# Output projection with head scales folded into the loaded operand, and the MLP's first operands made in pieces

## The chip, the core and the metric

The kernel runs on one core of one Trainium2 chip. The metric is the device time of one execution in microseconds (us). The core's engines run side by side, each through its own queue in order: TensorE (PE, with its weight loads PEld), VectorE (DVE), ScalarE (ACT), GpSimd (POOL), and SyncE (SP), which issues DMAs.

## The reference

One encoder block on 2048 tokens of width 1024, in float32: RMSNorm and input projection; on half of the width differential attention (4 heads), on the other half Fourier mixing; output projection with residual; RMSNorm and a gated MLP with a convolution over positions; a final RMSNorm. What concerns the change:

```python
o_da = diff_attention(q, k, v, lam, slopes)
o_da = rmsnorm(o_da, g_subln[l], SUBLN_EPS) * (1.0 - lambda_init)   # one scale per token and head
o_ft = fourier_mix(u, w_ft[l])
mixed = jnp.concatenate([o_da.reshape(B, S, DA_WIDTH), o_ft], axis=-1)
x = x + mixed @ w_out[l]
h = rmsnorm(x, g_ffn[l])
up = centred_dwconv(h @ w_up[l], w_conv[l], b_conv[l])
```

## The kernel before, in words

A product of float32 operands is made of three matmuls: `split` (L77) writes an operand as a high part (ACT) and a low part (a subtraction on DVE, or on POOL for the operand `ms`), and `mm3` (L119) runs high x high (L125), high x low (L126) and low x high (L127) into one PSUM bank.

**Attention** (L531) runs over 64 units, a head h and 128 queries i, in 4 steps t each. A step issues four score matmuls `s` (L567), four transposes `pt` (L598) of an earlier unit, and six value matmuls `o`. DVE takes the scores out of PSUM (L572), ACT makes the exponentials, POOL combines the two softmaxes (`combine`, L579: L441, L444 and two additions L589 for a unit). Two units are a pair `pr`. When a pair's `o` is complete, `finish` (L611) stores it unscaled in the DRAM tensor `mixed`, and two steps later makes the head scale: two matmuls with a column of ones (L624), a product on DVE (L629, `ft`), and on POOL L630, L631 (a power) and L632, which writes the column into the constant tile `fs` [token, head, block]. Nothing reads `fs` before the output projection. POOL also issues the loads of `q` (L504), one for every four units.

**The output projection** (`out_proj`, L693) runs over 16 blocks `tb` of 128 tokens. `load` (L709) brings a block of `mixed` (`mt`; half 1 is the Fourier part, half 0 the heads), splits it into `ms` (high on ACT, low on POOL), and brings the residual `x`. For each half of the output columns, `half` (L721) runs one group of 12 matmuls for the Fourier part (`of`), added by DVE (L733), and then four groups of three matmuls, one for each head (`o`), each added by DVE times that head's column of `fs` (L738). `close` (L741) of the block before makes the norm: square on ACT (L95), L98 and L100 on POOL (`h_rs`), product on DVE (L691, `hn`); its PE transposes (L754, `ht`) stand between the two parts of the next block's second half, and ACT copies (L758) and stores them in the DRAM tensor `htd`. `ms` has three buffers: the low part of a block's head half can be made only when the Fourier group of the block before has been run a second time.

**The MLP's first operands.** Its first group of products (tokens 0 to 1023) takes sums and differences of four quarters of `htd`, for four row groups `kb`. `b_part` (L806) makes them inside the output projection, after blocks 9, 11, 12 and 14: two loads of 512 KB into the one staging tile `hb`, four sums on POOL (L796 to L799), splits of four results into `b` (high ACT, low DVE) and copies of two on POOL into `held` (L825).

The order on each engine is not the order of the code alone: the framework places the instructions of independent parts by its own estimate of when each can start, and every engine then runs its list strictly in that order. A wait of an engine's head holds all that stands behind it.

Of the kernel before, what the change touches and what calls it, by code (L numbers as in the profile page):

```python
# [11 lines left out]
F32 = mybir.dt.float32  # L12
F32R = mybir.dt.float32r
# [7 lines left out]
P = 128  # L21
D = 1024
S = 2048
# [17 lines left out]
class Block:  # L41
# [3 lines left out]
    def __init__(self, ctx, tc, a):  # L45
# [22 lines left out]
        self.gd = dt("gd", [NF, P, S], F32)  # L68

# [461 lines left out]
    def attention(self, pss):  # L531

        nc, a = self.nc, self.a
        with ExitStack() as es:
# [98 lines left out]

            self.wo = {}
# [22 lines left out]
            for t in range(4 * (NU + LAG + 4)):  # L657
# [29 lines left out]


# [4 lines left out]
    def out_proj(self, big, operands):  # L693
# [3 lines left out]
        with ExitStack() as es:  # L697
# [11 lines left out]
            def load(tb):  # L709
                ms = []  # L710
                for half in (1, 0):
                    mt = p.tile([P, 4, P], F32, tag="mt", bufs=3, name=f"mt{tb}_{half}")
                    nc.sync.dma_start(mt, self.mixed[4 * half:4 * half + 4, :, tb * P:(tb + 1) * P].rearrange("k p t -> p k t"))
                    m2 = p.tile([P, 4, 2, P], F32R, tag="ms", bufs=3, name=f"ms{tb}_{half}")
                    self.split(mt, m2[:, :, 0, :], m2[:, :, 1, :], lo_engine=nc.gpsimd)
                    ms.insert(0, m2)
                x2 = p.tile([P, D], F32, tag="xh", name=f"x2_{tb}")
                nc.sync.dma_start(x2, a["x"][tb * P:(tb + 1) * P, :])
                ready[tb] = ms, x2

            def half(tb, half, between=None):  # L721
# [4 lines left out]

                def group(kbs, name):
                    ps = pso.tile([P, HALF], F32, tag="o", name=f"{name}{tb}_{half}")
                    return ps, self.mm3(ps, [term(kb) for kb in kbs])

                f = lambda h: self.fs[:, h, tb:tb + 1]
                ps, mm = group(range(H, KB), "of")
                nc.vector.tensor_tensor(x2[:, c], ps, x2[:, c], ALU.add)  # L733
                if between is not None:
                    between(mm)
                for h in range(H):
                    ps, _ = group([h], f"o{h}_")
                    last = nc.vector.scalar_tensor_tensor(x2[:, c], ps, f(h), x2[:, c], ALU.mult, ALU.add)  # L738
                return last

            def close(tb, behind=None):  # L741
                ms, x2 = ready.pop(tb)
                hn = p.tile([P, D], F32, tag="xh", name=f"hn{tb}")
                r = self.norm(p, hn, x2, gffn, f"h{tb}", hn)
                if behind is not None:
                    self.issue_after(r, behind)
# [59 lines left out]
    def b_part(self, grp, kb, out):  # L806

# [5 lines left out]
        for half in range(2):  # L813
# [5 lines left out]
        t1, t2, t3, t4 = self.sums(self.sp, (x11, x21, x12, x22), f"hs{grp}_{kb}",  # L819
                                   nc.vector if grp else nc.gpsimd, True)  # L820
        for o, v in zip(out, (x11, t1, t2, x21, t3, t4, x22)):
            if o is None:
                continue
            if len(o.shape) == 3:
                nc.gpsimd.tensor_copy(o[:, kb], v)  # L825
            else:
                self.split(v, o[:, 0, kb], o[:, 1, kb])
# [197 lines left out]
    def ffn(self, es_k):  # L1025
        nc, a = self.nc, self.a
        with ExitStack() as es:
# [6 lines left out]
            with ExitStack() as est:  # L1034
                late = self.pool(est, "late", 1)
                held = [late.tile([P, 4, HALF], F32, tag=f"h{i}", name=f"held{i}") for i in range(2)]
                self.out_proj(self.big, lambda step: self.b_part(0, step, self.bops + held + [None]) )
# [112 lines left out]
```

## Time and profile before

| what | us |
|---|---|
| median of 3 runs (2570.17 to 2577.55) | 2571.42 |
| the profiled execution's own time | 2574.7 |
| its span | 2572.9 |
| attention without Fourier work beside it | from about 440 to 979 |
| output projection | 979 to 1204 |

The profile page gives for each engine its busy time and share of the span, and the busy share in 40 slices of 64.3 us (a 9 is 90% or more). DVE is busy for 1752.6 us (68%), ACT for 1301.9 us (51%). Other views list instructions in order of time, who waited for whom, the chain of work that ended last, and busy times in chosen stretches. In a row `out<-in` names what an instruction writes and reads, buffer numbers left out; of a matmul's two operands the names are those of its operands, weights and moving data.

### The profile page before, as it was taken

What the parts mean: (1) busy time and instruction counts of PE and PEld (TensorE: products, weight loads), DVE (VectorE), ACT (ScalarE), POOL (GpSimd) and SP (SyncE); (2) the same over time, 40 slices, a digit from 0 to 9 for tenths busy, and PEclk for the clock granted to TensorE, in tenths of its full rate; (3) what the DMA queues carried; (4) which work ended last, traced back from release to release, by engine and by line L of the source; (5) the groups of instructions that cost most, each with busy time, mean ns of one, the idle gap of its engine ahead of it and who ended that gap; (6) DMA issues with size and microseconds to landing.
All of it is one profiled execution on the core that took longest, in us unless ns stands there. A gap on an engine that the chain in (4) does not pass through costs nothing.

```text
span 2572.9 us, 34950 instructions
## 1 busy us (share of the span) xinstructions
PE 2516.6 (98%) x13021; PEld 2114.6 (82%) x13021; DVE 1752.6 (68%) x2691; ACT 1301.9 (51%) x2036; POOL 716.9 (28%) x797
## 2 busy tenths in 40 slices
PE   9999999999999999978999999999999999999998
PEld 9998877888888888866888888877888888888886
DVE  4533358988889996786877777657777777434443
ACT  6321246888888883233544454444454445333332
POOL 1300015888988883271010010000000000000000
PEclk9999999999999999988999999999999999999999
DMA  8335558343332205554222221454212222546463
GB/s 264 98 125 139 152 143 237 66 74 73 74 75 50 48 26 173 181 174 140 107 74 79 88 79 70 160 181 155 91 74 76 88 83 85 185 137 219 146 204 113
DMA packets 146154, 309.12 MB, mean 120 GB/s; under 512 B 12080, under 2 KB 69440, under 8 KB 138816
## 3 DMA queue, kind: packets, MB, share of 16 engines
q1 hardware_dynamic: 90816, 226.60, 26.2%
q0 software_dynamic: 18256, 34.57, 6.7%
q10 hardware_dynamic: 36912, 45.72, 5.8%
q8 instruction: 102, 1.67, 0.3%
q14 instruction: 68, 0.56, 0.1%
HBM read 225.05 MB, written 81.80 MB: 119 GB/s over the span
## 4 chain that ended last, share of the span: by engine, by line
PE 87%; DVE 5%; DMA 4%; issue 1%; POOL 1%; ACT 1%; SPq 0%; POOLq 0%; ACTq 0%; DVEq 0%
PE s L567 9%; PE pd L127 5%; PE pd L125 5%; PE pd L126 5%; PE pt L598 4%; PE o L125 3%; PE o L127 3%; PE o L126 3%; PE pz L125 2%; PE pz L127 2%; PE pz L126 2%; DMA hb<-htd 2%; PE pv L127 1%; PE pv L126 1%; PE pv L125 1%
## 5 line engine op out<-in xcount | busy, mean ns | idle before, releaser
L589 POOL TENSOR_TENSOR z<-z,z 128x1024 f32<-128x1024 f32 x128 | 307.1, 2414 | 0.1
L82 DVE TENSOR_TENSOR d<-wd,d 128x512 fp32r<-128x512 f32 x240 | 157.0, 689 | 211.7 <-ACT d L81 211.4
L567 PE MATMUL s<-k,q 128*128 128x512 f32 x1024 | 281.5, 396 | 3.0 <-DVE mn L572 2.0
L576 ACT ACTIVATE z<-z,mn 128x2048 f32<-128x2048 f32 x128 | 257.5, 2012 | 33.7 <-DVE mn L572 32.7
L81 ACT ACTIVATE d<-wd 128x512 fp32r<-128x512 f32 x240 | 141.8, 626 | 236.9 <-PE pd L127 186.2
L125 PE MATMUL pd<-d,d 128*128 128x512 f32 x640 | 251.8, 393 | 1.9 <-ACT d L81 1.4
L127 PE MATMUL pd<-d,d 128*128 128x512 f32 x640 | 251.2, 393 | 0.5 <-DVE d L82 0.5
L126 PE MATMUL pd<-d,d 128*128 128x512 f32 x640 | 251.5, 393 | 0.0
L567 PEld LDWEIGHTS s<-k,q 128*128 128x128 f32 x1024 | 174.5, 188 | 29.4 <-DVE mn L572 5.0
L572 DVE CUSTOM_DVE_ANT_0 z<-s,dist,mn 128x1024 f32<-128x1024 f32 x128 | 163.8, 1280 | 38.6 <-PE s L567 37.8
L82 DVE TENSOR_TENSOR at<-pt,at 128x512 fp32r<-128x512 f32 x256 | 169.9, 686 | 8.5 <-ACT at L81 8.4
L81 ACT ACTIVATE at<-pt 128x512 fp32r<-128x512 f32 x256 | 147.5, 592 | 48.2 <-PE pt L598 44.8
L125 PE MATMUL o<-at,v 128*128 128x256 f32 x512 | 162.0, 316 | 0.0
L598 PE MATMUL pt<-ident,z 128*128 128x128 f32 x1024 | 156.7, 276 | 5.1 <-DVE at L82 5.1
L572 DVE CUSTOM_DVE_ANT_0 z<-s,dist 128x1024 f32<-128x1024 f32 x128 | 155.8, 1217 | 5.4 <-PE s L567 4.4
L598 PEld LDWEIGHTS pt<-ident,z 128*128 128x128 f32 x1024 | 125.7, 144 | 36.3 <-issue 10.5
L98 POOL TENSOR_SCALAR y_rs<-y_rs 128x1 f32<-128x1 f32 x16 | 6.9, 429 | 524.9 <-ACT sq L95 524.9
L126 PE MATMUL o<-at,v 128*128 128x256 f32 x512 | 146.3, 286 | 0.0
L125 PEld LDWEIGHTS pd<-d,d 128*128 128x128 f32 x640 | 120.1, 188 | 30.6 <-ACT d L81 1.8
L127 PEld LDWEIGHTS pd<-d,d 128*128 128x128 f32 x640 | 120.1, 188 | 29.0 <-DVE d L82 1.4
L127 PE MATMUL o<-at,v 128*128 128x256 f32 x512 | 143.7, 281 | 0.0
L126 PEld LDWEIGHTS pd<-d,d 128*128 128x128 f32 x640 | 120.1, 188 | 27.7 <-DVE d L82 0.3
(1058 smaller groups left out, 6895.0 us busy)
## 6 DMA issues: line engine op xcount, KB each, us to landing
wu<-in_w_up SPq DMA_DIRECT2D x44, 1024.0 KB, 4.8
wd<-in_w_down SPq DMA_DIRECT2D x88, 512.0 KB, 3.6
wd<-gd SPq DMA_DIRECT2D x88, 256.0 KB, 3.9
q<-qd POOLq DMA_DIRECT2D x32, 512.0 KB, 7.0
gd<-t SPq DMA_DIRECT2D x22, 512.5 KB, 2.6
gd<-t SPq DMA_DIRECT2D x22, 511.5 KB, 3.1
wst<-in_w_in SPq DMA_DIRECT2D x72, 128.0 KB, 3.6
xt<-in_xt SPq DMA_DIRECT2D x16, 512.0 KB, 4.6
```

The lines of the kernel that those rows point to most:

```text
L81: r = nc.scalar.activation(hi, src, AF.Copy)
L82: return r, (lo_engine or nc.vector).tensor_tensor(lo, src, hi.bitcast(F32), ALU.subtract)
L98: nc.gpsimd.tensor_scalar(t[:, 1:2], t[:, 0:1], 1.0 / D, EPS, ALU.mult, ALU.add)
L125: mm(ah, bh, start=first and i == 0, stop=False)
L126: mm(ah, bl, start=False, stop=False)
L127: r = mm(al, bh, start=False, stop=last and i == n - 1)
L567: nc.tensor.matmul(ps[:, j * HALF:(j + 1) * HALF], qt[:, 2 * c + l, i % 4 * P:i % 4 * P + P], kt[:, c, k0:k0 + HALF], start=l == 0, stop=l ...
L572: nc.vector.tensor_tensor_reduce(zt[:, half * 1024:(half + 1) * 1024], ps, dist[:, d0:d0 + 1024], SLOPES[h], 3.0e38 if half == 0 else mn[: ...
L576: nc.scalar.activation(zt, zt, AF.Exp, bias=mn[:, 2 * c + 1:2 * c + 2], scale=-1.0, accum_out=ss[:, c:c + 1])
L589: nc.gpsimd.tensor_tensor(z[:, x], z[:, x], z1[:, x], ALU.add)
L598: nc.tensor.transpose(pt[:, j * P:(j + 1) * P], zs[n, 0][:, kb * P:(kb + 1) * P], self.ident)
```

## The change

1. The scale rows. Behind every second pair, four columns of `fs` (four blocks of one head) are transposed on PE into a free part of that pair's PSUM bank, copied by DVE and stored by SP into a new DRAM tensor `fsd` [head, token]. The last four come in the output projection, at block 1.
2. `load` brings the four rows of `fsd` for its block to all partitions (`fr`, one buffer) and POOL multiplies `mt` of the heads by them before the split.
3. `half` runs all 24 matmuls into one bank and DVE adds it once; the 128 instructions of L738 are gone. `close` of the block before stands before the first half, and its norm no longer waits behind that half's last DVE instruction.
4. `b_part` for the first group becomes the generator `b_pieces`: loads, sums and splits in 14 pieces, one before and one behind each second half from block 9 on, and two staging tiles in turn. The sums of the first group stay on POOL.

```diff
+            def scale_rows(pr):
+                h, i = units[2 * pr]
+                if i % 4 == 2 and 2 * pr + 2 < NU:
+                    self.scale_rows(op, pos[pr][:, W + P:], h, i - 2)
...
+                if v >= 14 and (v - 14) % 8 == 0 and (v - 14) // 8 < NU // 2:
+                    scale_rows((v - 14) // 8)
...
+    def scale_rows(self, p, pt, h, i):
+        nc = self.nc
+        nc.tensor.transpose(pt[:4, :P], self.fs[:, h, i:i + 4], self.ident)
+        st = p.tile([4, P], F32, tag="fsr", bufs=1, name=f"fsr{h}_{i}")
+        nc.vector.tensor_copy(st, pt[:4, :P])
+        nc.sync.dma_start(self.fsd[h, i * P:(i + 4) * P].rearrange("(n p) -> n p", p=P), st)
...
+                    if half == 0:
+                        fr = p.tile([P, 4, P], F32, tag="fr", bufs=1, name=f"fr{tb}")
+                        nc.sync.dma_start(fr, self.fsd[:, c].partition_broadcast(P))
+                        nc.gpsimd.tensor_tensor(mt, mt, fr, ALU.mult)
...
-                ps, mm = group(range(H, KB), "of")
-                nc.vector.tensor_tensor(x2[:, c], ps, x2[:, c], ALU.add)
+                ps = pso.tile([P, HALF], F32, tag="o", name=f"o{tb}_{half}")
+                mm = self.mm3(ps, [term(kb) for kb in range(H, KB)], last=False)
                 if between is not None:
                     between(mm)
-                for h in range(H):
-                    ps, _ = group([h], f"o{h}_")
-                    last = nc.vector.scalar_tensor_tensor(x2[:, c], ps, f(h), x2[:, c], ALU.mult, ALU.add)
-                return last
+                self.mm3(ps, [term(kb) for kb in range(H)], first=False)
+                return nc.vector.tensor_tensor(x2[:, c], ps, x2[:, c], ALU.add)
...
             for tb in range(NB):
-                last = half(tb, 0)
-                transposes = close(tb - 1, last) if tb > 0 else None
+                transposes = close(tb - 1) if tb > 0 else None
+                half(tb, 0)
+                if tb == 1:
+                    self.scale_rows(p, pst.tile([P, HALF], F32, tag="tp", name="fsr"), H - 1, NB - 4)
                 if tb + 1 < NB:
                     load(tb + 1)
+                if tb > 8:
+                    next(pieces, None)
                 half(tb, 1, transposes)
-                if tb in (9, 11, 12, 14):
-                    operands((9, 11, 12, 14).index(tb))
+                if tb > 8:
+                    next(pieces, None)
...
+    def b_pieces(self, out):
...
+            for i in range(4):
+                nc.sync.dma_start(st[kb][i], self.htd[kb + 4 * (i % 2), :, i // 2 * HALF:(i // 2 + 1) * HALF])
+        load(0)
+        load(1)
+        yield
+        for kb in range(4):
+            x11, x21, x12, x22 = st[kb]
+            t1, t2, t3, t4 = self.sums(self.sp, (x11, x21, x12, x22), f"hs0_{kb}", nc.gpsimd, True)
+            yield
+            for n, (o, v) in enumerate(zip(out, (x11, t1, t2, x21, t3, t4))):
+                if n == 3:
+                    yield
+                if len(o.shape) == 3:
+                    nc.gpsimd.tensor_copy(o[:, kb], v)
+                else:
+                    self.split(v, o[:, 0, kb], o[:, 1, kb])
+            if kb + 2 < 4:
+                load(kb + 2)
+            yield
```

How the instructions stand on the engines, at three places. Lines of the changed kernel are one or more higher than those of before for the same statement (L598 is L599, L82 is L83, L796 to L799 are L813 to L816, L825 is L865).

First PE in attention, at the step where a second pair's rows are taken (here pair 3). Before:

```order
L567 MATMUL s_00_5489<-k_4054,q_3_5179 128x512 x4
L125 MATMUL o_5350<-at_3_5272,v_4314 128x256
L598 MATMUL pt_0_5495<-ident,z_0_5288 128x128 x4
L126 MATMUL o_5350<-at_3_5272,v_4314 128x256
L127 MATMUL o_5350<-at_3_5272,v_4314 128x256
```

And now:

```order
L568 MATMUL s_00_5494<-k_4055,q_3_5184 128x512 x4
L699 MATMUL o_5152<-ident,fs 4x128
L599 MATMUL pt_0_5504<-ident,z_0_5293 128x128 x4
L126 MATMUL o_5355<-at_3_5277,v_4315 128x256
L127 MATMUL o_5355<-at_3_5277,v_4315 128x256
```

The transpose of `fs` (L699) stands directly behind the four score matmuls of that step, ahead of the transposes and of everything else on PE; it reads the column that POOL's L632 (now L633) wrote for the same pair. There are 15 such places, all with the same neighbours but the last.

Second PE where the output projection begins, now:

```order
L128 MATMUL o_10844<-at_3_10779,v_8350 128x256
L625 MATMUL o_10844<-ones,osq_10910 128x1 x2
L699 MATMUL fsr<-ident,fs 4x128
L126 MATMUL o_0_10983<-wo_x_9177,ms_1_10970 128x512
L127 MATMUL o_0_10983<-wo_x_9177,ms_1_10970 128x512
L128 MATMUL o_0_10983<-wo_x_9177,ms_1_10970 128x512
```

The sixteenth transpose stands here, though the code has it at block 1: behind the last two ones matmuls (L625) and ahead of the first matmul of the output projection. Before, the ones matmuls were followed by that matmul.

Third POOL, from the norm of block 8 (`h_rs`) on. The low part of the head half of block 10 is `ms_0_11871` before and `ms_0_11818` now. Before:

```order
L100 TENSOR_TENSOR h_rs<-h_rs,mhalf 128x1
L796 TENSOR_TENSOR hs_0_t_11929<-hb_0_11926 128x512
L797 TENSOR_TENSOR hs_0_t_11930<-hb_0_11926,hs_0_t_11929 128x512
L798 TENSOR_TENSOR hb_0_11926<-hb_0_11926 128x512
L799 TENSOR_TENSOR hs_0_t_11931<-hb_0_11926,hs_0_t_11930 128x512
L825 COPY held_10884<-hb_0_11926 128x512
L825 COPY held_10885<-hs_0_t_11931 128x512
L82 TENSOR_TENSOR ms_0_11871<-mt_0_11869,ms_0_11871 128x4x128
```

And now, from the third sum of row group 0 on (the first two stand directly ahead):

```order
L815 TENSOR_TENSOR hb_0_11823<-hb_0_11823 128x512
L816 TENSOR_TENSOR hs_0_t_11878<-hb_0_11823,hs_0_t_11877 128x512
L865 COPY held_10945<-hb_0_11823 128x512
L734 TENSOR_TENSOR mt_0_11921<-mt_0_11921,fr_11923 128x512
L865 COPY held_10946<-hs_0_t_11878 128x512
L813 TENSOR_TENSOR hs_1_t_12036<-hb_11_11829,hb_10_11828 128x512
L814 TENSOR_TENSOR hs_1_t_12037<-hb_11_11829,hs_1_t_12036 128x512
L815 TENSOR_TENSOR hb_11_11829<-hb_11_11829 128x512
L816 TENSOR_TENSOR hs_1_t_12038<-hb_10_11828,hs_1_t_12037 128x512
L865 COPY held_10945<-hb_11_11829 128x512
L83 TENSOR_TENSOR ms_0_11818<-mt_0_11813,ms_0_11818 128x4x128
```

Twelve instructions (two row groups' sums, three copies and the product for block 11) now stand between the norm of block 8 and block 10's low part, where six stood before. Behind it follow a copy, the four sums of row group 2, the low part of block 11's Fourier half, two copies, and only then the norm of block 9; then, with the product for block 12 among them, the four sums and two copies of row group 3, and the low part of block 11's head half. The pieces that the code hands out over blocks 9 to 15 thus stand on POOL in blocks 9 to 11.

More of the change, by code (lines that the diff above doesn't have):

```diff
@@ L691, in norm, with out_proj @@
         return self.nc.vector.scalar_tensor_tensor(hn, x2, r, gain, ALU.mult, ALU.mult)
-    def out_proj(self, big, operands):
+    def out_proj(self, pieces):
         nc, a = self.nc, self.a
@@ L725, in half, with close @@
                                    wo[kb][:, 0, c], wo[kb][:, 1, c])
[L727 to L731, printed above, removed]
-                ps, mm = group(range(H, KB), "of")
-                nc.vector.tensor_tensor(x2[:, c], ps, x2[:, c], ALU.add)
+                ps = pso.tile([P, HALF], F32, tag="o", name=f"o{tb}_{half}")
+                mm = self.mm3(ps, [term(kb) for kb in range(H, KB)], last=False)
                 if between is not None:
                     between(mm)
-                for h in range(H):
-                    ps, _ = group([h], f"o{h}_")
-                    last = nc.vector.scalar_tensor_tensor(x2[:, c], ps, f(h), x2[:, c], ALU.mult, ALU.add)
-                return last
-            def close(tb, behind=None):
+                self.mm3(ps, [term(kb) for kb in range(H)], first=False)
+                return nc.vector.tensor_tensor(x2[:, c], ps, x2[:, c], ALU.add)
+            def close(tb):
                 ms, x2 = ready.pop(tb)
                 hn = p.tile([P, D], F32, tag="xh", name=f"hn{tb}")
-                r = self.norm(p, hn, x2, gffn, f"h{tb}", hn)
-                if behind is not None:
-                    self.issue_after(r, behind)
+                self.norm(p, hn, x2, gffn, f"h{tb}", hn)
                 nc.scalar.dma_start(self.x2d[tb], x2)
@@ L817, in b_part, with load @@
         x11, x21, x12, x22 = (st[:, i] for i in range(4))
-        t1, t2, t3, t4 = self.sums(self.sp, (x11, x21, x12, x22), f"hs{grp}_{kb}",
-                                   nc.vector if grp else nc.gpsimd, True)
+        t1, t2, t3, t4 = self.sums(self.sp, (x11, x21, x12, x22), f"hs{grp}_{kb}", nc.vector, True)
         for o, v in zip(out, (x11, t1, t2, x21, t3, t4, x22)):
[L822 to L825, printed above, removed]
-            else:
-                self.split(v, o[:, 0, kb], o[:, 1, kb])
+            self.split(v, o[:, 0, kb], o[:, 1, kb])
+    def b_pieces(self, out):
+        nc = self.nc
+        st = {}
+        def load(kb):
+            if kb % 2 == 0:
+                t = self.sp.tile([P, 4, HALF], F32, tag="st", bufs=1, name=f"hb0_{kb}")
+                st[kb] = [t[:, i] for i in range(4)]
+            else:
+                t = [self.sp.tile([P, 2, HALF], F32, tag=f"a{i}", bufs=1, name=f"hb0_{kb}{i}") for i in range(2)]
+                st[kb] = [t[i // 2][:, i % 2] for i in range(4)]
+            for i in range(4):
[13 more added lines that the diff above has]
+                else:
+                    self.split(v, o[:, 0, kb], o[:, 1, kb])
+            if kb + 2 < 4:
+                load(kb + 2)
+            yield
     def stage(self, name):
```

10 lines of the change are left out of this document (7 added, 3 removed).

## Prediction

> **What bounds the kernel now.** I read the page first. Columns: engine, busy time, share of the span, instructions; below, busy tenths in slices of 64.3 us.
>
> ```profile
> PE 2516.6 (98%) x13021; PEld 2114.6 (82%) x13021; DVE 1752.6 (68%) x2691; ACT 1301.9 (51%) x2036; POOL 716.9 (28%) x797
> PE   9999999999999999978999999999999999999998
> POOL 1300015888988883271010010000000000000000
> ```
>
> PE is the bound, and full in all but a few slices. So an edit gains only where PE stands still, and loses wherever it makes PE stand still. PE's holes (7 and 8) lie in the second part of the output projection. Attention (slices 7 to 15) has none, and POOL is busiest there. The busy times by stretch cut the output projection in two (stretch, length, PE, PEld, DVE, ACT, POOL, granted clock, DMA share, GB/s):
>
> ```profile
> 979.00:1087.00 108.00, 108.00 (x500) 87.43 (x500) 76.20 (x100) 29.41 (x52) 30.57 (x37) 1.00 0.54 164
> 1087.00:1204.00 117.00, 94.05 (x398) 75.66 (x397) 86.08 (x102) 35.20 (x60) 55.34 (x56) 0.90 0.52 164
> ```
>
> Until block 9 PE has no hole, whatever DVE does. After that it loses 23 us, and its clock falls to 0.90. The chain of work that ended last, in order of time, tells how much and why:
>
> ```profile
> 1011.05 0.90 PE ht L754 x8
> ...
> 1071.38 0.90 PE ht L754 x8
> ...
> 1085.16 3.80 DMA htd<-hs
> 1088.97 6.57 DMA hb<-htd
> ...
> 1194.46 0.89 PE ht L754 x8
> ```
>
> The transposes of successive blocks stand one period apart: five periods from 1011.05 to 1071.38, so 12.07 us for a block, or (12.07 - 0.90) / 48 = 0.233 for a matmul. The next eight take 123.08 instead of 96.5: **26.5 us is all that the operand work costs there**, stops and half clock together. The path goes through `hb`, loaded 3.8 + 6.57 us after block 7 is stored, then through POOL and ACT queues that hold `ms` and `hn` behind the sums.
>
> **Part by part.** *Head scales out of the evictions.* These groups are from the output projection:
>
> ```profile
> L738 DVE SCALAR_TENSOR_TENSOR x<-o,fs,x 128x512 f32<-128x512 f32 x128 | 95.9, 749 | 19.4 <-PE o L127 9.0
> L691 DVE SCALAR_TENSOR_TENSOR hn<-x,h_rs,gffn 128x1024 f32<-128x1024 f32 x16 | 23.3, 1456 | 2.3 <-POOL xg L892 2.2
> ```
>
> DVE loses 95.9 us of work. I cost this at nothing: in the first stretch PE ran 108.00 of 108.00 us beside it, so PE was its cover and there was no stop to recover. PE still has 24 matmuls a half; fewer PSUM groups change no count.
>
> *Scale rows in attention.* Fifteen times PE takes a transpose of `fs` right behind the score matmuls, and waits there for POOL's L632 of the same pair. The list in order of time, at pairs 1, 2, 3, 23 and 27 (start, duration); the PE rows are what PE did next after those scores:
>
> ```profile
> 485.99 0.60 PE L598 MATMUL pt<-ident,z 128*128 128x128 f32 x4
> 488.01 0.18 POOL L632 TENSOR_TENSOR fs<-ft,rr 128x2 f32<-128x2 f32 x1
> ...
> 498.55 0.20 POOL L632 TENSOR_TENSOR fs<-ft,rr 128x2 f32<-128x2 f32 x1
> 503.13 0.28 PE L125 MATMUL o<-at,v 128*128 128x256 f32 x1
> ...
> 520.21 0.28 PE L125 MATMUL o<-at,v 128*128 128x256 f32 x1
> 521.40 0.18 POOL L632 TENSOR_TENSOR fs<-ft,rr 128x2 f32<-128x2 f32 x1
> ...
> 862.44 0.28 PE L125 MATMUL o<-at,v 128*128 128x256 f32 x1
> 864.75 0.18 POOL L632 TENSOR_TENSOR fs<-ft,rr 128x2 f32<-128x2 f32 x1
> ...
> 930.76 0.28 PE L125 MATMUL o<-at,v 128*128 128x256 f32 x1
> 926.19 0.19 POOL L632 TENSOR_TENSOR fs<-ft,rr 128x2 f32<-128x2 f32 x1
> ```
>
> At pair 3 the column is ready at 521.58, and PE is there at 520.21: **1.37 us late**. Even pairs have it early (pair 2: 498.75 for 503.13), but the rows are taken at odd ones, where L632 stands behind POOL's `q` loads and two additions. Thirteen of the fifteen are late: ten like pair 3 (1.2 to 1.4), pair 1 by 2.2, pair 21 by 1.8, pair 23 by 2.5; pairs 27 and 29, after the last `q` load, are not. Sum, pair by pair in the same list: 13.2 + 6.5 = 19.7. Does POOL catch up after a stop, so that the next is shorter? Two groups of attention:
>
> ```profile
> L441 POOL TENSOR_SCALAR z<-z,cf 128x1024 f32<-128x1024 f32 x62 | 69.8, 1127 | 48.9 <-DVE cf L585 48.0 <-DVE ft L629 0.3
> L572 DVE CUSTOM_DVE_ANT_0 z<-s,dist,mn 128x1024 f32<-128x1024 f32 x121 | 154.9, 1280 | 38.3 <-PE s L567 37.8
> ```
>
> POOL stands idle 48.0 us for DVE's `cf`, and DVE 37.8 us for PE's scores: both follow PE, so a PE delay moves them along and the lateness comes back each time. PE works without slack here, so each stop moves the end. The transposes add 15 x 0.11 (0.90 for eight), with weight loads about 2. Term A = **+22**. Bounds: 14, if `cf` comes 0.5 earlier relative to PE because DVE gains room; 26, if the two longest stops also cost clock. The DVE copy and the tiny SP store behind each transpose stand behind PE and hold nothing PE needs within 4 us.
>
> *Clock.* These stretches hold a stop and what follows it:
>
> ```profile
> 1094.00:1098.50 4.50, 2.68 (x12) 1.86 (x11) 4.50 (x6) 2.42 (x4) 3.15 (x3) 1.00 0.30 100
> 1098.50:1101.90 3.40, 3.39 (x19) 2.95 (x20) 3.40 (x5) 1.72 (x3) 3.40 (x3) 1.00 0.64 200
> ...
> 1147.60:1149.90 2.30, 0.05 (x2) 0.05 (x1) 2.25 (x4) 0.89 (x2) 1.45 (x3) 1.00 0.31 121
> 1150.00:1153.40 3.40, 3.40 (x14) 2.91 (x14) 3.25 (x4) 2.12 (x4) 3.40 (x3) 0.58 0.50 152
> ```
>
> A stop of 1.8 us (4.50 - 2.68) left the clock at 1.00; one of 2.25 was followed by 0.58 over 3.4 us, which costs about 1.4 to 1.7. So I give the 1.4 us stops no clock cost. The Trainium skill ("TensorE: Matmul & The Clock Gate", section "HAM oscillation — how this bites in real kernels") names idle gaps over about 3.4 us as the ones to avoid; by it no stop of attention would cost clock, so term A would end at 22 and the half-clock rival below would have no chance. This trace disagrees at 2.25 us, and the measurement decides.
>
> *The beginning of the output projection.* Its first matmul now stands behind a transpose that needs the last `fs`:
>
> ```profile
> 974.01 1.29 POOL L82 TENSOR_TENSOR ms<-mt,ms 128x512 fp32r<-128x512 f32 x1 [1.46 <-ACT ms L81]
> ...
> 979.17 0.48 PE L125 MATMUL of<-wo_x,ms 128*128 128x512 f32 x1
> ...
> 981.09 0.20 POOL L632 TENSOR_TENSOR fs<-ft,rr 128x2 f32<-128x2 f32 x1
> ```
>
> PE stops from 979.17 to 981.3. POOL made block 0's low parts at 974 before; now they stand behind that L632, with the product between: low part 1.3, product 1.3 (priced like L82, two inputs of 128x512), ACT's high part 0.6, low part 1.3, so 981.3 + 4.6 = 985.9. PE needs it 14 matmuls in, at 979.17 + 3.26 = 982.4. Term B = **+4** (3.5, and some chance of a slow clock; 2 to 6).
>
> *The pieces.* POOL's prices, by group:
>
> ```profile
> L82 POOL TENSOR_TENSOR ms<-mt,ms 128x512 fp32r<-128x512 f32 x30 | 39.6, 1323 | 93.8 <-ACT ms L81 93.7
> L100 POOL TENSOR_TENSOR h_rs<-h_rs,mhalf 128x1 f32<-128x1 f32 x16 | 8.7, 542 | 1.3
> L798 POOL TENSOR_TENSOR hb<-hb 128x512 f32<-128x512 f32 x4 | 8.5, 2124 | 0.0
> L799 POOL TENSOR_TENSOR hs_t<-hb,hs_t 128x512 f32<-128x512 f32 x4 | 6.9, 1728 | 0.0
> L797 POOL TENSOR_TENSOR hs_t<-hb,hs_t 128x512 f32<-128x512 f32 x4 | 5.8, 1453 | 2.1 <-DMA hb<-htd 2.1
> L796 POOL TENSOR_TENSOR hs_t<-hb 128x512 f32<-128x512 f32 x4 | 5.1, 1282 | 18.7 <-DMA hb<-htd 18.7
> L825 POOL COPY held<-hb 128x512 f32<-128x512 f32 x4 | 4.3, 1075 | 0.0
> ...
> L825 POOL COPY held<-hs_t 128x512 f32<-128x512 f32 x4 | 2.4, 608 | 0.0
> ```
>
> Count from block 9's first matmul (near 1087 before). The last quarter of row group 0 lands at about 7.5 (8.5 for both halves before, from the chain above). Then POOL does, as the order has it, eleven instructions and block 10's low part: 17.3 us at these means, 13.4 at the cheapest rows, 1.28 for each sum and 0.61 for each copy; so at 20.9 to 24.8, middle 22.9. PE needs it at 12.07 + 3.26 = 15.3: a stop of about 7.6. Next, a copy, four sums, a low part, two copies and the norm of block 9 take 9.1 to 11, then 1.46 on DVE (L691): PE gets its transposes at 34.4 instead of 20.5, 13.9 late in all. Then row group 3's four sums and two copies, a product and block 11's low part (9 to 10.9) bring another 1 to 2. Later blocks have a free POOL. With a little half clock: **16.5 late in place of 26.5** (12 to 21). Term C = **-10** (-14.5 to -5.5).
>
> DVE's load decides where in that range. The Trainium skill ("GPSIMD Engine Reference", section "Key points") says that POOL shares its SBUF interfaces with DVE and is held up by DVE instructions in a 2-port mode or with two SBUF inputs. The removed L738 read PSUM and `x`; the low parts of `b` have two SBUF inputs and stay, so by that rule the sums keep their long times, C is -5.5 and the whole +20.5 instead of +16. The rows 1282 and 2124 for like sums fit contention, but do not show with whom.
>
> *Costed at nothing.* The 16 loads of `fr` (256 KB each) and the hoisted `hb` loads ride on a DMA share of 0.54; `mt` and `x` are fetched a block ahead, 12 us of cover for landings of 4; were that cover gone, each late block would cost its lateness. The stop at the end, where the last norm's chain (add, square, power, product) precedes PE's transposes, stays as it was.
>
> **The sum.** 22 + 4 - 10 = +16. Against the profiled execution's own 2574.7 (1.8 around its span) that is 2590.7; the median of the runs is 3.3 lower, so I predict **2587**, slower by 0.6%. Ends: 14 + 2 - 14.5 = +1.5 and 26 + 6 - 5.5 = +26.5, so 2573 to 2598.
>
> **Rivals.**
> - *POOL is in time in attention*: its timing shifts, or DVE's room pulls `cf` forward by more than 1.4. Then A is 2, and the sum 2 + 4 - 10 = -4: 2567. For: the even pairs are over 4 early. Against: POOL's list there is the same as before, and waits for PE.
> - *The output projection runs clean* from block 9 on, A as forecast: 22 + 4 - 26.5 = -0.5: 2571, not slower. It needs POOL's twelve instructions in under 7.8 us (15.3 - 7.5), or 0.65 each, half the cheapest sum's price. For: quarters of `hb` arrive earlier. Against: every row above.
> - *Both*: 2 + 4 - 26.5 = -20.5: 2551, faster. That is what it does if it does what it says.
> - *Half clock in attention*: every late transpose pulls the clock down for 3.4 us, 1.7 each: 16 + 13 x 1.7 = +38: 2609. For: 2.25 us did. Against: 1.8 did not.
> - *The edit is not spread*: the pieces lie in blocks 9 to 11, not 9 to 15; this is in the forecast.
>
> **How the numbers follow.** Forecast 0.70, POOL in time 0.08, clean projection 0.10, both 0.05, half clock 0.07. A measurement of this kernel can tell about 0.3% (7.7 us) from no change: 2563.7 to 2579.1. "Same" takes the first two rivals and 0.03 of the forecast's low end; "faster" takes "both" and 0.01; the rest is slower. The range reaches below to the clean projection and above past the forecast's end: 2570 to 2603.
>
> **What would show it.** A: about 13 PE stops of 1 to 2.5 us at the `fs` transposes released by POOL, attention some 22 us longer. B: one stop of 2 us on the sixteenth, then PE waiting for `ms`. C: two long PE stops in blocks 10 to 11, one at `ms` behind POOL, one at `ht` behind `hn`; none from block 12 on. I am wrong if attention keeps its length, or if block 10 starts its heads' matmuls without a stop.

## Result and the profile after

The changed kernel takes 2642.0 us (median of 4 runs, 2638.93 to 2644.85) beside 2570.8 for the kernel before (4 runs, 2568.63 to 2577.55): a ratio of 1.0272, 95% interval 1.0249 to 1.0295. It is slower, as predicted, but by 71 us where 16 were forecast. The page of the changed kernel, the lines that answer to those of before, and of its fourth part the shares of the chain that ended last:

```profile
PE 2531.7 (96%) x13037; PEld 2120.5 (80%) x13037; DVE 1662.3 (63%) x2579; ACT 1304.1 (49%) x2036; POOL 731.8 (28%) x813
PE   9999999999999998868999999999999999999998
POOL 1300015888887883354010100100000000000000
PE 71%; DMA 9%; POOL 7%; DVE 5%; issue 5%; ACT 2%; SPq 0%; POOLq 0%; ACTq 0%; DVEq 0%
PE s L568 4%; PE pd L126 4%; PE pd L128 4%; PE pd L127 4%; DMA fr<-fsd 4%; POOL z L590 3%; PE pz L128 2%; PE pz L126 2%; PE pz L127 2%; PE pt L599 2%; PE o L128 1%; PE o L126 1%; DMA hb<-htd 1%; PE o L127 1%; DVE z L573 1%
```

DVE lost 90 us of work (1752.6 to 1662.3). PE's holes have become deeper, and a name that was not in the chain of before stands in it now: the load `fr<-fsd`, 4% of 2639, some 100 us of waiting. The busy times by stretch, for the output projection cut where block 9 begins, as in the prediction (stretch, length, PE, PEld, DVE, ACT, POOL, granted clock, DMA share, GB/s):

```profile
1004.00:1140.60 136.60, 116.70 (x498) 91.70 (x498) 26.99 (x31) 30.61 (x55) 43.49 (x45) 0.93 0.55 149
1140.60:1273.00 132.40, 96.21 (x398) 75.51 (x397) 38.99 (x42) 31.63 (x56) 59.12 (x63) 0.86 0.50 157
```

The first stretch was 108 us with PE full; it now takes 136.6, with 19.9 in which PE stands still and a granted clock of 0.93 instead of 1.00, before any operand piece is made (POOL's first sum starts at 1159.7). The DMA share is what it was (0.55 for 0.54). Where the output projection begins and ends, PE's rows (start, duration, what, in brackets the time that PE stood idle before it and what released it): the sixteenth transpose of `fs`, behind which the projection's first matmul stands, and the last norm's transposes, of the changed kernel and (last row) of before:

```profile
1003.89 0.27 PE L699 MATMUL fsr<-ident,fs 128*4 128x128 f32 x1 [1.68 <-POOL fs L633]
...
1271.90 0.48 PE L765 MATMUL ht<-ident,hn 128*128 128x128 f32 x1 [4.19 <-DVE hn L707]
```

```profile
1202.91 0.47 PE L754 MATMUL ht<-ident,hn 128*128 128x128 f32 x1 [4.79 <-DVE hn L691]
```

The output projection began with its first matmul at 979.17 and now begins at 1004.16, the end of that transpose (1003.89 + 0.27): 25.0 later. From there to the last transposes were 223.7 us and are 267.7: 44.0 more. What follows is 2.8 shorter (1370.0 and 1367.2 to the spans' ends). The sum is the 66.2 between the two spans.

What does the projection wait for? The chain of waits of the changed kernel from the product of block 4 to the rows of block 6, in order of time (start, duration, what):

```profile
1052.55 1.31 POOL mt L734
1053.86 0.02 issue
1053.87 10.70 DMA fr<-fsd
1064.57 0.02 issue
1064.60 0.02 POOLq L734
1064.61 3.99 issue
1068.60 0.02 POOLq L83
1068.62 0.02 issue
1068.64 1.27 POOL mt L734
1069.91 0.02 issue
1069.93 9.49 DMA fr<-fsd
```

PE is not in it. One product of the scale rows (L734) releases the next load of the rows, the load takes about 10 us, the product waits on for `mt`, loaded behind it on the same queue, and so on: 16.1 us from product to product here, 15.2 on average over blocks 3 to 10, where PE needs 12.07 for a block. The group of that product says the same of the whole projection (after the bar: busy, mean ns of one, idle time before them and its cause):

```profile
L734 POOL TENSOR_TENSOR mt<-mt,fr 128x512 f32<-128x512 f32 x16 | 22.3, 1395 | 110.4 <-DMA mt<-mixed 85.7 <-DMA fr<-fsd 14.2 <-DMA htd<-hs 10.5
```

Most of these waits end with `mt` and not with the rows, because a block's `mt` stands behind its rows on the queue.

### The profile page after: what moved, and what is told of

It reads as the page before. It is cut to its first block, busy times and chain, and to the rows that moved or that the text cites. A ratio compares the mean times of both kernels' runs of the same rounds, so it can differ in the third digit from the quotient of the medians.

```text
span 2639.1 us, 34824 instructions
## 1 busy us (share of the span) xinstructions
PE 2531.7 (96%) x13037; PEld 2120.5 (80%) x13037; DVE 1662.3 (63%) x2579; ACT 1304.1 (49%) x2036; POOL 731.8 (28%) x813
## 4 chain that ended last, share of the span: by engine, by line
PE 71%; DMA 9%; POOL 7%; DVE 5%; issue 5%; ACT 2%; SPq 0%; POOLq 0%; ACTq 0%; DVEq 0%
PE s L568 4%; PE pd L126 4%; PE pd L128 4%; PE pd L127 4%; DMA fr<-fsd 4%; POOL z L590 3%; PE pz L128 2%; PE pz L126 2%; PE pz L127 2%; PE pt L599 2%; PE o L128 1%; PE o L126 1%; DMA hb<-htd 1%; PE o L127 1%; DVE z L573 1%
## 5 line engine op out<-in xcount | busy, mean ns | idle before, releaser
L83 DVE TENSOR_TENSOR d<-wd,d 128x512 fp32r<-128x512 f32 x240 | 156.7, 688 | 211.5 <-ACT d L82 211.2
L82 ACT ACTIVATE d<-wd 128x512 fp32r<-128x512 f32 x240 | 141.6, 625 | 236.6 <-PE pd L128 176.1
L83 DVE TENSOR_TENSOR at<-pt,at 128x512 fp32r<-128x512 f32 x256 | 169.9, 685 | 12.2 <-ACT at L82 11.9
L82 ACT ACTIVATE at<-pt 128x512 fp32r<-128x512 f32 x256 | 147.7, 591 | 59.8 <-PE pt L599 56.4
L599 PE MATMUL pt<-ident,z 128*128 128x128 f32 x1024 | 156.6, 276 | 4.1 <-DVE at L83 3.6
L599 PEld LDWEIGHTS pt<-ident,z 128*128 128x128 f32 x1024 | 125.6, 144 | 32.9 <-issue 7.1
L127 PEld LDWEIGHTS pd<-d,d 128*128 128x128 f32 x640 | 120.1, 188 | 27.5
```

What stands on the lines that cost most here:

```text
L82: r = nc.scalar.activation(hi, src, AF.Copy)
L83: return r, (lo_engine or nc.vector).tensor_tensor(lo, src, hi.bitcast(F32), ALU.subtract)
L127: mm(ah, bl, start=False, stop=False)
L599: nc.tensor.transpose(pt[:, j * P:(j + 1) * P], zs[n, 0][:, kb * P:(kb + 1) * P], self.ident)
```

## The experiments

All are edits of the changed kernel unless said otherwise. The theory: the load of the rows (256 KB a block, which the prediction cost at nothing) is slow, and its chain is longer than a block. Rivals: the added bytes, POOL's added work, the pieces.

**1. The same load from another place, by another queue, and no load.**

The other source (the heads are then multiplied by rows of `mixed` in place of their scales):

```diff
-                        nc.sync.dma_start(fr, self.fsd[:, c].partition_broadcast(P))
+                        nc.sync.dma_start(fr, self.mixed[0:4, :, c].rearrange("k p t -> p k t"))
```

> The load of the scale rows reads 256 KB of the mixed heads instead, in as many packets of 512 B, all from different places; so the heads are scaled by wrong numbers. Theory A (slow because 512 packets read the same 2 KB): the load lands in about 4 us like mt instead of 8 to 11, blocks 2 to 8 return to 12.1 us, and some 40 us of the 43 in the output projection go: 2600 to 2608. Theory B (any further 256 KB a block on this queue with one buffer costs it): landing stays at 8 to 11 us, 2636 to 2646. Theory C (POOL's product and the operand pieces hold the projection up): no change either, but with the landing at 4.

Measured: 2590.92 (2588.39 to 2591.74).

No load, with a constant tile made once ahead of the loop in place of the scales:

```diff
+            fr = w.tile([P, 4, P], F32, name="fr")
+            nc.gpsimd.memset(fr, 0.5)
...
-                        fr = p.tile([P, 4, P], F32, tag="fr", bufs=1, name=f"fr{tb}")
-                        nc.sync.dma_start(fr, self.fsd[:, c].partition_broadcast(P))
```

> The scale rows aren't loaded: the product takes a constant tile, made once. Transposes and stores of the rows stay, and so does POOL's product. If the load is the whole excess of the output projection over what was predicted: 2642 less 40 to 55, so 2587 to 2602, near the predicted 2587 plus the longer end of attention. If POOL's product and the pieces are what costs: 2630 or more.

Measured: 2591.04 (2590.43 to 2591.62).

The change's own load from ACT's queue:

```diff
-                        nc.sync.dma_start(fr, self.fsd[:, c].partition_broadcast(P))
+                        nc.scalar.dma_start(fr, self.fsd[:, c].partition_broadcast(P))
```

> The load of the scale rows is issued by ACT instead of SP; same bytes, same place read, one buffer still. Theory A' (what costs is that mt and x stand behind the slow load on SP's queue: 10 + 3.4 + 2 x 2.5 to 3.8 is over a block's 12.1 us): the loads overlap, a loop of 10 for the load and 1.3 for the product fits in 12.1, blocks near 12.1 again: 2598 to 2612. Theory B' (the DMA engines' capacity, whichever queue): within 8 of 2642. Rival: ACT's own work waits behind the issue, which waits for POOL's product: 2625 to 2650.

Measured: 2645.73 (2642.87 to 2650.17).

So the load from `fsd` costs 51 us, and neither its bytes nor its 512 packets nor POOL's product are the cause: the same number of bytes and packets from other places costs no more than not loading at all (2590.9 for 2591.0). That is more than the 44 us by which the projection is longer than before, because without the slow load it is some 7 us shorter than before. On ACT's queue nothing is won. The chain of that run shows why: now `mt`, on a queue without the rows, is what is late. Its rows, and the issue of a load of the scale rows on ACT's queue less than 5 us ahead of the second of them:

```profile
1038.96 8.67 DMA mt<-mixed
1053.75 8.38 DMA mt<-mixed
1068.10 9.03 DMA mt<-mixed
```

```profile
1049.08 0.37 ACTq L733 DMA_DIRECT2D fr<-fsd  x1
```

A load of `mt` took 3.8 us before (median from issue to landing; its row stands further down). The Trainium skill ("DMA: Bandwidth & Descriptors", section "Queues, rings and completion order") says that SP's and ACT's queues are rings on the same 16 DMA engines, which take turns between them. The rows agree: the slow load holds up a quick one on the other queue.

**2. A second buffer.** Blocks 1, 3, 5 and 7 load into a tile that is free until block 9.

```diff
-                        fr = p.tile([P, 4, P], F32, tag="fr", bufs=1, name=f"fr{tb}")
+                        fr = self.sp.tile([P, 4, HALF], F32, tag="st", bufs=1, name=f"fr{tb}")[:, 0].rearrange("p (k t) -> p k t", k=4) \
+                            if tb % 2 and tb < 8 else p.tile([P, 4, P], F32, tag="fr", bufs=1, name=f"fr{tb}")
```

> The change, with a second place for the scale rows in blocks 1, 3, 5 and 7 (a tile that is free until block 9), so that the load of a block need not wait for the product of the block before; reads as slow as in the change. If the loop over the one buffer sets the 15 us of a block: blocks 2 to 8 return to 12 to 13 us, 2618 to 2626. If the queue itself is full (slow rows 6, x 3.5, the two mt 1.3 to 2 each, and what ACT stores meanwhile): blocks stay at 14 to 15 us, 2633 to 2645.

Measured: 2640.73 (2639.51 to 2645.20). The single buffer alone is not the limit. Between 1028 and 1067 us the chain of this run goes through `mt` (7.9 to 9.3 us a load) instead of the rows: the slow load of the next block only moves ahead in the same engines.

**3. Why the load is slow.** All with the same 256 KB a block; copies of the rows, or another distance between the four heads' rows in DRAM. The edit for the rows stored by block is this; the others differ in the shape of `fsd`, which the table gives, and in the store and load that fit it:

```diff
-        self.fsd = dt("fsd", [H, S], F32)
+        self.fsd = dt("fsd", [NB, H, P], F32)
...
-        nc.sync.dma_start(self.fsd[h, i * P:(i + 4) * P].rearrange("(n p) -> n p", p=P), st)
+        nc.sync.dma_start(self.fsd[i:i + 4, h], st)
...
-                        nc.sync.dma_start(fr, self.fsd[:, c].partition_broadcast(P))
+                        nc.sync.dma_start(fr, self.fsd[tb].partition_broadcast(P))
```

> The change, with the scale rows stored four times in DRAM, 32 KB apart, and each group of 32 partitions loading its own copy: the same bytes, the same 512-B packets, the same broadcast, but 32 reads of each place instead of 128. Theory A (reads of one place are served one after the other): the load lands in about 4 us, 2590 to 2602. Rival (a broadcast over partitions is slow as such, or four issues on SP cost as much): 2630 to 2646.

> The change, with the load of the scale rows reading four rows of the mixed heads that lie 1 MB apart, each still for all 128 partitions (so the heads are scaled by wrong numbers): 512 packets of 512 B, four places, the four far apart instead of 8 KB. If the small distance was the trouble (four copies 32 KB apart hardly helped): landing about 4 us, 2588 to 2600. If it is 128 reads of one place, however far apart the places are: landing 7 to 11 us, 2630 to 2646.

> The change, with the scale rows stored 128 times, so that each partition reads a copy of its own, 32 KB from the next: the same bytes in the same 512 packets of 512 B, nothing read twice. If reads of few places are what is slow: landing about 4 us, 2588 to 2600. If the small tensor's place in DRAM or a load from it so soon after its store is slow: 2630 or more.

> The change, with the scale rows stored block by block, so that the four rows of a block lie together and each partition reads them in one packet of 2 KB: the same bytes and the same broadcast from one place, in 128 packets instead of 512. If what is slow is the number of reads of one place: landing near the 3.5 us of the row load of the same 256 KB in the input projection, which also reads 2 KB for 128 partitions; 2588 to 2600, as with the load from other places (2590.9). If it is the bytes read from one place: 2630 to 2646.

> The change, with the four rows of a block stored 640 B apart instead of 8 KB: 512 packets of 512 B again, four places, 128 reads of each. If it is going to and fro between places 8 KB apart that is slow: x starts 2 to 3 us after the load's issue, not 6, and 2588 to 2600. If it is the number of small reads from within a few KB (1 MB apart it was not slow, in one packet of 2 KB neither): 6 us and 2630 to 2646.

> The change, with the scale rows of the heads 8.5 KB apart instead of 8 KB: everything else the same. If a distance of a power of two is the trouble: x 2 to 3 us after the issue, 2588 to 2600. If any such distance is: 6 us, 2630 to 2646.

> The change, with the scale rows of the heads 64 KB apart instead of 8 KB. 640 B, 8.5 KB and 1 MB were not slow. If every small multiple of 8 KB is slow (four copies 32 KB apart were): 2630 to 2646, a load waits 7 to 9 us. If only 8 KB itself is: 2590 to 2600, about 4 us.

> The change, with the scale rows of the heads 2 KB apart (four blocks' rows together). If small powers of two are slow: 2630 to 2646. If the slow distance begins higher, between 2 and 8 KB: 2590 to 2600.

The third column is read from the trace's DMA packets: `x` stands directly behind the rows in SP's queue, and the time from the issue of the rows to the first packet of `x` is a measure of how long the rows hold the queue (smallest to largest of 11 or 12 blocks; the blocks in which `x` was issued later for another reason are left out). The times are medians of four runs (the change, four copies, one packet, experiment 1) or of two.

| rows of a block stored as | places x distance | us until `x` starts | median us |
|---|---|---|---|
| the change, `fsd [H, S]` | 4 x 8 KB | 5.5 to 8.1 | 2642.0 |
| four copies, `fsd [4, H, S]` | 16 x 8 KB | not read (four loads) | 2632.4 |
| `fsd [H, 8 * S]` | 4 x 64 KB | 3.9 to 7.0 | 2615.1 |
| `fsd [H, S + P]` | 4 x 8.5 KB | 2.1 to 3.8 | 2596.5 |
| `fsd [NB // 4, H, 4 * P]` | 4 x 2 KB | 2.0 to 3.7 | 2593.9 |
| `fsd [NB, H, 160]` | 4 x 640 B | 2.2 to 3.9 | 2592.9 |
| `fsd [NB, H, P]`, one packet of 2 KB a partition | 1 | 2.0 to 4.2 | 2593.7 |
| rows of `mixed` in place of the scales | 4 x 1 MB | 2.2 to 3.2 | 2594.1 |
| a copy for each partition, `fsd [P, H, S]` | 512 x 8 KB | 2.1 to 3.2, once 7.9 | 2601.9 |
| `mixed`, other source (experiment 1) | 512 x 8 KB | 1.8 to 2.1 | 2590.9 |

The same can be seen on POOL. Each pair is SP's issue and the product that waited for that load, in the change, at 640 B and at 8.5 KB (in brackets the wait):

```profile
1017.68 0.36 SPq L733 DMA_DIRECT2D fr<-fsd  x1
1025.54 1.26 POOL L734 TENSOR_TENSOR mt<-mt,fr 128x512 f32<-128x512 f32 x1 [7.88 <-DMA fr<-fsd]
```

```profile
1011.72 0.36 SPq L733 DMA_DIRECT2D fr<-fsd  x1
1015.66 1.29 POOL L734 TENSOR_TENSOR mt<-mt,fr 128x512 f32<-128x512 f32 x1 [3.97 <-DMA fr<-fsd]
```

```profile
1013.14 0.36 SPq L733 DMA_DIRECT2D fr<-fsd  x1
1016.65 1.30 POOL L734 TENSOR_TENSOR mt<-mt,fr 128x512 f32<-128x512 f32 x1 [3.54 <-DMA fr<-fsd]
```

From issue to product a load takes 7.9 us at 8 KB, 3.9 at 640 B and 3.5 at 8.5 KB, with the same 512 packets of 512 B. So it isn't the broadcast, nor 128 reads of one place, nor small packets: it is **four 512-B rows at 8 KB from each other**. At 64 KB the kernel loses about half as much (2615.1, between 2593 and 2642). My expectation for the four copies was wrong in that light: they too lie at multiples of 8 KB. Not every such layout is slow (1 MB is not, nor are 512 places 8 KB apart); what in the memory does this stays open. Where the whole tensor lies in DRAM was not varied by itself.

**4. The transposes in attention, one pair later.**

```diff
-                h, i = units[2 * pr]
-                if i % 4 == 2 and 2 * pr + 2 < NU:
+                h, i = units[2 * pr - 2]
+                if pr > 0 and i % 4 == 2:
                     self.scale_rows(op, pos[pr][:, W + P:], h, i - 2)
```

> The change, with each transpose of the scale columns in attention taken one pair (8 steps) later, when POOL's result is long there. Term A (PE waits there for POOL): the 13 stops, 16.8 us in the trace of the change, go, and 2642 becomes 2625 (2620 to 2630). Rival (the stops only use up slack, and the time is lost at the next score or at the start of the projection): 2636 to 2644.

Measured: 2634.56 (2633.33 to 2637.38). All stops at L699 in attention are gone, and the sixteenth transpose ends, and with that the projection begins, at 985.16, 19.0 earlier than in the change. But the projection is 9.4 longer: it still hangs on the slow loads, and has stops that the change doesn't have, 1.3 us at its first matmul and this one:

```profile
996.86 0.80 PE L126 MATMUL o<-wo_x,ms 128*128 128x512 f32 x1 [5.39 <-ACT ms L82]
```

The expectation was 10 us too low because it took the gain in one stage for a gain at the end, while the next stage was not bound by PE.

**5. Each part alone.** First the pieces, with `close` ahead of the first half as in the change; rows and product go, and the evictions of before return:

```diff
-                        nc.gpsimd.tensor_tensor(mt, mt, fr, ALU.mult)
...
-                self.mm3(ps, [term(kb) for kb in range(H)], first=False)
-                return nc.vector.tensor_tensor(x2[:, c], ps, x2[:, c], ALU.add)
+                for h in range(H):
+                    ps, _ = group([h], f"o{h}_")
+                    last = nc.vector.scalar_tensor_tensor(x2[:, c], ps, f(h), x2[:, c], ALU.mult, ALU.add)
+                return last
```

> The scales stay in the evictions as before (no transposes, no rows, no product); the MLP's first operands are made in small pieces, close before the half block, as in the change. By the prediction's third term: 10 less than before, 2561 (2556 to 2566). Rival (the pieces are as bad as the old parts, and only the load made the difference in the change): 2567 to 2575. Rival (the pieces cost more): over 2578.

Measured: 2563.51 (2558.74 to 2565.25), ratio 0.9967 (0.9955 to 0.9978): a gain of 7.7.

Then the scales, with `b_part` and its four places as before:

```diff
-                self.out_proj(self.b_pieces(self.bops + held))
+                self.out_proj(self.big, lambda step: self.b_part(0, step, self.bops + held + [None]) )
```

> The scales go into the operand as in the change; the MLP's first operands are made in the old way (one part behind blocks 9, 11, 12 and 14). If the parts add: 2642 plus the 7.7 that the pieces alone gained, 2650 (2643 to 2658). If the slow load of the rows covers whatever the operands cost, both ways the same: 2638 to 2645.

Measured: 2662.99 (2660.20 to 2663.99). Outside what was expected: the parts don't add. Beside the late `ms` the old parts cost more than they did before: four stops of 10.6, 12.4, 10.7 and 6.1 us at the norm's transposes, where the longest was 5.6 before. What each of these stops hangs on was not followed.

**6. Better versions.** In the pieces alone POOL still runs ahead: it makes sums of the next row group before a block's own low part and norm. The edit (on the pieces alone) orders the first sum and the copies of each row group behind the last low part that POOL made for `ms`:

```diff
-                    self.split(mt, m2[:, :, 0, :], m2[:, :, 1, :], lo_engine=nc.gpsimd)
+                    _, self.lo_op = self.split(mt, m2[:, :, 0, :], m2[:, :, 1, :], lo_engine=nc.gpsimd)
...
-            t1, t2, t3, t4 = self.sums(self.sp, (x11, x21, x12, x22), f"hs0_{kb}", nc.gpsimd, True)
+            t1, t2, t3, t4 = self.sums(self.sp, (x11, x21, x12, x22), f"hs0_{kb}", nc.gpsimd, True, self.lo_op)
...
-                    nc.gpsimd.tensor_copy(o[:, kb], v)
+                    self.issue_after(nc.gpsimd.tensor_copy(o[:, kb], v), self.lo_op)
```

> The pieces alone (scales in the evictions as before), and each piece's first POOL instruction ordered behind POOL's last low part of the block, so that POOL never makes two pieces ahead of a block's own work. The pieces alone have stops of 0.9, 3.6, 6.3, 0.3 and 0.3 us in blocks 9 to 13 and 10.2 us at half clock behind them: 2563.5 less 11 to 16, 2547 to 2553. Rival (DVE, with evictions and low parts, is the one that is late): 2558 to 2566.

Measured: 2554.27 (2553.45 to 2556.50), ratio 0.9938 (0.9922 to 0.9955). It beats both kernels; 2547 to 2553 was expected. By stretch:

```profile
980.80:1088.90 108.10, 108.10 (x501) 88.44 (x502) 77.34 (x104) 31.79 (x56) 30.92 (x37) 1.00 0.58 176
1088.90:1185.70 96.80, 86.80 (x398) 69.32 (x397) 74.76 (x98) 31.91 (x56) 50.55 (x56) 0.97 0.63 187
```

The second stretch takes 96.8 where before it took 117.0 (23 of them without PE). Of its 10.0 us of stops 8.5 are one, at the end:

```profile
1184.61 0.47 PE L766 MATMUL ht<-ident,hn 128*128 128x128 f32 x1 [8.53 <-DVE hn L705]
```

The next run orders the MLP's first weight sums behind the last norm on DVE:

```diff
-            v["p5"], v["p6"], v["p7"], v["p3"] = self.sums(self.sp, [st[:, i] for i in range(4)], f"ws{grp}_{n}", nc.vector)
+            v["p5"], v["p6"], v["p7"], v["p3"] = self.sums(self.sp, [st[:, i] for i in range(4)], f"ws{grp}_{n}", nc.vector,
+                behind=self.hn_op if (grp, n) == (0, 0) else None)
```

> The paced pieces, with the first sums of the MLP's weights ordered behind the last norm on DVE, since in the paced run four of them stand between the last evictions and PE's last stop is 8.5 us instead of 4.8. If they are what makes the last evictions late: that stop returns to 5 to 6 us, 2550 to 2552. If the sums are then late for the MLP's first product: 2554 or more.

Measured: 2554.10 (2549.41 to 2556.36), the last stop 6.8 instead of 8.5 (5 to 6 was expected): no difference in time that can be measured.

Last the change with its losses mended, the edits of 4, of 6 (pacing) and of the rows stored by block together:

> The change with its three losses taken out together: rows stored by block, transposes one pair later, pieces ordered behind each block's own POOL work. From 2590.9 (the load from other places): 17 less for the attention stops and 12 to 18 for the stops of blocks 10 to 12 with the half clock behind them, so 2556 to 2564. If a repaired head scale gained on PE at all, it would end under the paced pieces with the old evictions (2554.3); if the start of the projection stays late by the 2 to 4 us of term B, just above.

Measured: 2570.31 (2564.89 to 2573.04), ratio 0.9992 (0.9982 to 1.0001). Above what was expected, and 16 us above the paced pieces with the old evictions. From the rows stored by block (2593.7) its projection begins 20.7 us earlier, but is only 5.1 shorter: it keeps stops at the norm's transposes (2.8, 1.2 and 3.4 us). What these hang on was not followed. A repaired head scale therefore gains nothing over none at all: it takes 90 us from an engine that held nobody up. Of the 16.6 us by which its profiled execution is longer than that of the paced pieces (spans of 2568.3 and 2551.7), 3.7 lie ahead of the projection's first matmul, with the transposes, 8.3 in the projection and 4.6 behind it.

## Why the prediction was right in its direction and wrong in its size

*Evictions at nothing: right.* DVE got 90 us lighter, and in each pair of versions that differ by this part, and by the scale rows that go with it, the one with it is slower: 2662.99 and 2571.24 with the old parts, 2593.65 (rows by block) and 2563.51 with the pieces, 2570.31 and 2554.27 with the paced pieces.

*Scale rows in attention, +22: right.* PE stops at 13 of the 15 transposes, released by POOL's L633 (three of them, at pairs 3, 13 and 25):

```profile
525.11 0.27 PE L699 MATMUL o<-ident,fs 128*4 128x128 f32 x1 [1.23 <-POOL fs L633]
...
702.96 0.27 PE L699 MATMUL o<-ident,fs 128*4 128x128 f32 x1 [1.24 <-POOL fs L633]
...
918.12 0.27 PE L699 MATMUL o<-ident,fs 128*4 128x128 f32 x1 [1.25 <-POOL fs L633]
```

The thirteen sum to 16.9 (19.7 was read off, with 2.5 at pair 23, which measured 1.2); the lateness came back each time, as argued. At the last score matmuls of attention PE is 21.7 us later than before. Of that 1.3 was there from the scores at 410 us on, ahead of the first transpose (the paced pieces, which have no transposes, are 2.1 later there, so this is a difference between executions). So attention cost 20.4, of which 3.5 lie outside the thirteen stops, where 2 was given; with the stops gone (experiment 4) it still costs 3.1. No stop at these transposes was followed by a lower clock in the change, so the rival with half clock did not happen.

*The beginning of the projection, +4: right in size, by another way.* From the last scores to the beginning of the projection PE falls 3.3 us further behind, to the 25.0. The stop at the sixteenth transpose is there (1.7; 2 was forecast), but the wait for `ms`, on which the term was built, came to 0.3 in the change. Instead PE runs at a granted clock of 0.50 for 10.2 us at the end of attention (987.2 to 997.4), where it was 6.8 before (966.2 to 973.0), and again from 1004.3 to 1007.7, so that it needs `ms` later. That the sum is met is in part luck. The medians confirm the two terms together: the change without the load (2591.0) is 27.5 above the pieces alone (2563.5); 26 was forecast.

*The pieces, -10: right once the load is mended.* PE's rows in the run with the rows stored by block:

```profile
1005.38 0.27 PE L699 MATMUL fsr<-ident,fs 128*4 128x128 f32 x1 [1.68 <-POOL fs L633]
...
1134.75 0.80 PE L126 MATMUL o<-wo_x,ms 128*128 128x512 f32 x1 [4.88 <-ACT ms L82]
...
1139.14 0.79 PE L128 MATMUL o<-wo_x,ms 128*128 128x512 f32 x1 [3.17 <-POOL ms L83]
...
1150.38 0.47 PE L765 MATMUL ht<-ident,hn 128*128 128x128 f32 x1 [4.53 <-DVE hn L707]
...
1222.34 0.47 PE L765 MATMUL ht<-ident,hn 128*128 128x128 f32 x1 [4.19 <-DVE hn L707]
```

The stops come at `ms` and at `ht` behind `hn` in block 10, a small one in block 11, and the transposes from block 12 on stand 12.0 to 12.1 us apart until the last. The projection takes 216.7 (1005.65 to 1222.34) where it took 223.7: -7.0 for -10. With +26.5 ahead of it, and 0.3 less behind it, this run's span is the 19.1 longer that 2592.0 and 2572.9 differ by; the medians differ by 22 (2593.65 and 2571.45); +16 was forecast. The sums did not keep their long times, as the working from the Trainium skill's rule on POOL's shared interfaces had it ("GPSIMD Engine Reference", section "Key points"): `hb`'s sum fell from 2.25 to 1.5 us (medians) in the pieces, with the evictions gone and with them kept alike. So the evictions are not what held POOL up; whether anything else on DVE did, no run here shows.

*The failed step: "Costed at nothing. The 16 loads of `fr` (256 KB each) ... ride on a DMA share of 0.54".* They cost 51 us. Two things were wrong in it. The cover was not there: "`mt` and `x` are fetched a block ahead, 12 us of cover for landings of 4" was true of the kernel before, but `fr` has one buffer and is issued only when the product of the block before has run, with `x` and `mt` behind it in the queue. At 4 us a load that chain still fits into a block of 12.07, as the runs with other distances show, so this alone would have cost nothing; and experiment 2, which gives four blocks their cover back, wins nothing. The other thing was the price, and this is what cost the time: the load takes 8 to 11 us, not the 4 of `mt`, because of where the four rows lie, and it slows `mt` beside it. Nothing in the trace of before showed that. Its list of DMAs (tile, engine, count, size, median us to landing) has, beside `mt`, a load of the same size that also brings one row to all partitions, from a single place of 2 KB:

```profile
mt<-mixed SPq DMA_DIRECT2D x32, 256.0 KB, 3.8
...
row<-rsd SPq DMA_DIRECT2D x16, 256.0 KB, 3.5
```

They would have confirmed the wrong price. But the step said what happens if the cover is gone ("each late block would cost its lateness") and gave no number to it: as an estimate from rows of before, with a load twice as long as `mt` (L82 for the product, the landings of `mt` and `x`, and 1.3 or more for each `mt` behind them) the chain of product, rows, `x` and two `mt` is 1.3 + 8 + 3.4 + 2 x 1.3, over 15 us, 3 more than a block, some 45 over the projection. That belonged among the rivals, with a time near 2632.

## What to carry to other kernels

A DMA share of 0.54 says that there is room, not that the next load will land as the others do: for a load of a new shape, write down what releases it, what stands behind it in its queue, add the durations up to the next release, and give the case in which it takes twice as long its own price. Where several rows are read by all partitions, store them so that one packet brings them, or away from the distances that were slow here (8 and 64 KB), and measure that load by itself. Work taken from an engine that holds nobody up gained nothing; making POOL's work in pieces and ordering them behind each block's own gained 17 us here without taking anything away.

## What the runs showed of the hardware that was not expected

- Of a load of 256 KB in 512 packets of 512 B, read from four places by all partitions, the time went with the distance of the places: the load behind it started 6.4 us after its issue at 8 KB, 5.4 at 64 KB and 2.4 to 3.0 at 640 B, 2 KB, 8.5 KB and 1 MB (medians over the blocks). The Trainium skill ("DMA: Bandwidth & Descriptors", section "Specifications") names 512 B as the least transfer for line rate. All these loads have packets of that size, so here the size alone does not tell how long a load takes.
- Such a load slows others on the same DMA engines, whichever queue they are in: with it on ACT's queue, `mt` took 8.4 to 9.0 us in the rows above instead of 3.8, at a mean DMA share of 0.54 (1004 to 1140 us of that run).
- The same stop lowers the granted clock in some executions and not in others. Fourteen of the profiled executions have the stop at the first late transpose (2.00 to 2.05 us); in five of them a stretch of 3.4 us at half clock begins 0.1 to 1.4 us behind it, in nine none does. None of the twelve shorter stops (1.1 to 1.7 us) in each of these has one behind it. These are the stretches behind the first stop in the run with four copies and in the change:

```profile
489.50:492.90 3.40, 3.01 (x13) 2.88 (x14) 0.62 (x3) 1.36 (x4) 2.35 (x6) 0.58 0.04 10
```

```profile
489.50:492.90 3.40, 3.40 (x26) 3.18 (x27) 1.69 (x4) 1.82 (x3) 2.36 (x4) 1.00 0.02 8
```

The clock was 0.58 behind a stop of 2.00 us, and 1.00 behind one of 2.04.
